# Three chunks of half products in the first MLP product of layer 0 as well, modulation pieces moved, and an output projection that opens four groups

## The chip, the cores and the metric

One core of a Trainium2 chip runs the whole program in one launch. The metric is the device time of a run in microseconds. TensorE (PE in the views) multiplies, VectorE (DVE) and ScalarE (ACT) do the work around it, GpSimd (POOL) issues some transfers, and SyncE (SP) issues the weight transfers.

## What is computed

The reference is one step of a two-layer backbone over 128 context tokens and 512 latent tokens, together T = 640 columns, with 1024 features. Cut to the parts that matter here:

```python
def layer(x, mod, lp, ...):
    shift1, scale1, gate1, shift2, scale2, gate2 = jnp.split(mod, N_MOD, axis=-1)
    hn = rmsnorm(x, lp['norm_w'][0]) * (1.0 + scale1) + shift1
    y, k, v, hs = mixer(hn, lp, ...)          # four head groups, then @ lp['w_out']
    x = x + gate1 * y
    hn = rmsnorm(x, lp['norm_w'][1]) * (1.0 + scale2) + shift2
    x = x + gate2 * (jnp.square(jax.nn.relu(hn @ lp['w_mlp1'])) @ lp['w_mlp2'])
```

`mod` comes from a product of a conditioning vector with `w_ada` (1024 x 6144) in each layer; `w_mlp1` is 1024 x 4096 and `w_mlp2` is 4096 x 1024. All of it is float32.

## The kernel before

**Layout.** Activations stand with features on the 128 partitions and the 640 tokens along the free axis, cut in two halves A and B, mostly 320 each. A float32 product is made of three matmuls in a reduced format: both sides are split into a high part and a remainder (`wh`, `wl` for weights; `hh`, `hl` for the normed activations), and high by high, remainder by high and high by remainder are added up in PSUM. One group is 8 slices of 128 features by 3, which is 24 matmuls of 320 columns (`group`, L768). ScalarE makes `wh` (L269, L314) and VectorE the remainder `wl` (L252), both for 128x1024 elements at a time.

**Stages.** Layers are numbered 0 and 1 in the code and here. After the mixers and the output projection (`g_L_o`), the MLP runs in four chunks q of 1024 inner features: a first product (MLP1, 16 groups, with squares by ScalarE and VectorE at L1460 to L1465), then its share of the second product (MLP2, 16 groups `g_L_0A` to `g_L_1B`, added to `x` by VectorE at L1404).

**Half products.** For the chunks in `FAST`, which are q = 1, 2, 3 of layer 1, `fast_mlp1` (L391) replaces four quarter products by seven products of sums: each pair of weight blocks needs 14 x 24 instead of 16 x 24 matmuls over the chunk (L432). `sums_gen` (L332) makes the sums of the activations once in a layer, after the first MLP1 chunk: for each of four slices there are twelve VectorE operations on 128x320 elements (the sums at L354 and L373 to L385, and remainders at L360 and L363) and four ScalarE casts. `sum_and_split` (L297) makes the sums of the weights, with an addition on VectorE (L311) before some of the splits. The products' results are added by VectorE at L450.

**Modulation.** The vector `mod` of layer 0's last third and of all of layer 1 is made on VectorE in passes over pieces of `w_ada` (`ada_dve`, L488 and L490): a piece is 512 KB and takes four passes of 128x512. There are 56 such pieces in the MLP of layer 0.

**Order of the work.** `run` writes a list of weight pieces in the order of their use, with modulation pieces among them. Five staging buffers `st` (`WST`) and four pairs `wh`, `wl` are in turn; a transfer on SyncE starts when a staging buffer is done with. In each chunk of layer 0 the pieces are dealt out so:

```python
n = 2 if q else AQ[b]          # behind each of four MLP1 weight blocks; AQ = (0, 1, 3, 5)
...
it += nxt[ni:ni + 2]           # behind each of four MLP2 weight blocks
```

The scheduler turns this into one fixed queue for each engine; an engine works through its queue in order. PSUM has two rotating banks for groups (`gp`), a tile `S` of three banks, and `TA`, `TB` and `U`. The output projection starts when two groups can be open; the last mixer outputs `y` that it needs come from VectorE and from a small product at L1244.

Of the kernel before, what the change touches and what calls it, by code (L numbers as in the profile page):

```python
# [9 lines left out]
F32 = mybir.dt.float32  # L10
F32R = mybir.dt.float32r
# [29 lines left out]
AQ = (0, 1, 3, 5)  # L41
AP1 = {"xr": (0, 8), "xb": (8, 16)}
WST = 5
FAST = {(1, 1), (1, 2), (1, 3)}
RP = 645
XC = 642
UP = 643
# [69 lines left out]
class Net:  # L117
# [30 lines left out]
    def setup_consts(self, consts):  # L148
        nc, c = self.nc, self.const
        self.cst = c.tile([P, 164], F32, name="cst")  # L150
        nc.scalar.dma_start(self.cst, consts[:, 0:164])
        self.ident = self.cst[:, 0:128]
        self.inv = self.cst[:, 128:130]
        self.edge = self.cst[:, 130:162].rearrange("p (f j) -> p f j", f=2)
        self.consts = consts
        self.sel = c.tile([P, 2], F32, name="sel")
        selv = self.cst[:, 0:128].rearrange("p (j r) -> p r j", j=4)[:, 0:2, :]
        nc.vector.reduce_sum(self.sel, selv, AX.X)
        self.ones = c.tile([P, P], F32, name="ones")
# [9 lines left out]
        self.rgw = c.tile([P, 8, P], F32, name="rgw")  # L169
# [162 lines left out]
    def sums_gen(self):  # L332
# [2 lines left out]
            yield  # L335
        self.vsbS.put(self.vsb)
        self.osbS.put(self.osb)
        o, v, qk = self.osbS.get(F32R), self.vsbS.get(F32R), self.qk.get(F32R)
        ms = [self.m.get(F32R) for _ in range(5)]
        self.sum_own = (o, v, qk, ms)  # L340
        of, vf = o.rearrange("p a b -> p (a b)"), v.rearrange("p a b -> p (a b)")
        cut = lambda t, k: t[:, HC * k:HC * k + HC]
        T1 = [(cut(of, k), cut(vf, k)) for k in range(4)]
        T2 = [(cut(qk, k), cut(qk, 4 + k) if k < 3 else cut(ms[4], 0)) for k in range(4)]
        T4 = [(cut(ms[k // 2], k % 2), cut(ms[2 + k // 2], k % 2)) for k in range(4)]
# [44 lines left out]

    def fast_mlp1(self, l, q, put):  # L391
        nc = self.nc
        self.until(lambda: self.summed and self.psS.ok() and self.psB.ok() and self.pt.ok(2), "sums")
        S, tb = self.psS.get(), self.psB.get()
        g = [self.gp.tile([P, 512], F32, tag="g", name=f"f{q}_{i}") for i in range(2)]
        pairs = [(g[0], g[1]), (S[:, 0:512], S[:, 512:1024]), (S[:, 1024:1536], tb)]
        t1, t5 = self.pt.get(), self.pt.get()
        half = lambda t, mi: t[:, HC * mi:HC * mi + HC]
        left = {}

        def finish(m, c, r, mi, sign):
            hi, lo = put(m, c)
            v = half(r, mi)

            def late():
# [6 lines left out]
                left[id(r)] -= 1  # L412
                if not left[id(r)]:
                    self.e.put(r)

            self.spawn(late(), first=True)

        for b in range(2):
            Y, Z, X = pairs[b % 3], pairs[(b + 1) % 3], pairs[(b + 2) % 3]
            r = u2 = None  # L420
            for prod, bank in ((1, Y), (5, Z), (6, Y), (3, Z), (2, X), (7, Y), (4, Y)):
# [4 lines left out]
                for mi in range(2):  # L426
# [33 lines left out]
        self.pt.put(t1, t5)  # L460
        self.psS.put(S)
        self.psB.put(tb)

    def sums_done(self):
        o, v, qk, ms = self.sum_own
        self.osbS.put(o)
        self.vsbS.put(v)
        self.qk.put(qk)
        self.m.put(*ms)
        self.vsb, self.osb = self.vsbS.get(), self.osbS.get()  # L470

    def ada_dve(self, l, s, g, kp):
        nc = self.nc
# [285 lines left out]
    def group(self, W, mi, mov, korder, ncols, nm):  # L759
# [3 lines left out]
        for i, k in enumerate(korder):  # L763
# [507 lines left out]
    def layer(self, l, last):  # L1271
# [118 lines left out]
        self.until(lambda: len(self.y) == 8 and not self.gens, "mixers")  # L1390
        self.mix_done = True
        self.until(lambda: (l, 1) in self.ada_done)

        self.until(lambda: self.m.ok(2), "acc")
        acc, rr = self.m.get(), self.m.get()
# [29 lines left out]
        self.gemm(self.order([(L, "o", b) for b in range(4)], lambda i: i == 2), mov_y,  # L1425
                  lambda key, mi, c, pt: ev(key, mi, c, pt, fin1), pre=lambda i: self.until(lambda: (l, 2, 0) in self.ada_done) if i == 12 else None)
# [20 lines left out]
        for q in range(4):  # L1447
# [288 lines left out]
    def run(self):  # L1736
# [3 lines left out]
        for l in range(DEPTH):  # L1740
# [71 lines left out]
```

## Time and profile before

| what | value |
| --- | --- |
| median of 3 runs | 1458.77 us (1457.07 to 1461.47) |
| the profiled execution's own time | 1458.18 us |
| its span, first to last instruction | 1456.4 us |
| TensorE busy | 98% of the span |
| VectorE busy | 69% |
| ScalarE busy | 44% |

A row of the views names the line, the engine, the operation, the tile written, and the tiles read. Busy time is what an engine's instructions cover; an instruction's duration can overlap the start of the next on its engine. In a chain each piece is what the next one waited for.

### The profile page before, as it was taken

To read this page: it belongs to the slowest core of one execution; us is meant where nothing else is said; L and a number is where in the kernel's file an instruction comes from. 1 tells how busy PE (TensorE), PEld (TensorE's weight loads), DVE (VectorE), ACT (ScalarE), POOL (GpSimd) and SP (SyncE) were. 2 spreads that over 40 slices of the span, in tenths; PEclk is the share of its full clock that TensorE was granted. 3 is DMA by queue.
4 is the path that set the end of the run, shared out by engine and by line. 5 is a ranking of instruction groups with operands and counts; after the bars stand their busy time and mean duration, and the time that the engine had idled before them with its cause. 6 is when DMAs were issued, how large, how long until landed. Compare 5 with 4: busy or idle time off the path is not lost.

```text
span 1456.4 us, 24564 instructions
## 1 busy us (share of the span) xinstructions
PE 1434.4 (98%) x9847; PEld 1367.7 (94%) x9847; DVE 998.6 (69%) x1924; ACT 643.7 (44%) x1195; POOL 60.9 (4%) x104
## 2 busy tenths in 40 slices
PE   8999999999999999999999999999999999999998
PEld 6877989999999999999999999899999999999997
DVE  5565989898886686866359768947594644644653
ACT  5535794363124123214346577625442722722731
POOL 1121010010000000000002200000000000000000
PEclk8999999999999999999999999999999999999999
DMA  9686214535553543543224601221222432432401
GB/s 333 195 220 186 79 43 97 159 95 175 176 186 115 161 146 117 177 147 122 74 78 127 155 30 59 44 73 59 88 85 79 143 104 74 148 106 77 151 23 73
DMA packets 145465, 174.02 MB, mean 119 GB/s; under 512 B 10500, under 2 KB 120536, under 8 KB 145352
## 3 DMA queue, kind: packets, MB, share of 16 engines
q1 hardware_dynamic: 140760, 165.85, 37.2%
q0 software_dynamic: 4224, 6.45, 2.0%
q8 instruction: 77, 1.26, 0.4%
q14 instruction: 36, 0.29, 0.1%
q10 hardware_dynamic: 368, 0.16, 0.0%
HBM read 159.84 MB, written 3.15 MB: 112 GB/s over the span
## 4 chain that ended last, share of the span: by engine, by line
PE 88%; DVE 5%; DMA 3%; ACT 2%; issue 1%; SPq 0%; DVEq 0%; ACTq 0%
PE g_L_0A L768 13%; PE g_L_1A L768 13%; PE g_L_0B L768 12%; PE g_L_1B L768 12%; PE S L432 4%; PE g_L_o_0B L768 2%; PE g_L_o_1B L768 2%; PE g_L_v L1361 2%; PE g_L_o_0A L768 2%; DMA st<-in_w_mlp 2%; PE g_L_o_1A L768 2%; PE f L432 2%; PE TB L1025 1%; PE S L978 1%; PE U L1133 1%; PE U L289 1%
## 5 line engine op out<-in xcount | busy, mean ns | idle before, releaser
L252 DVE TENSOR_TENSOR wl<-st,wh 128x1024 fp32r<-128x1024 f32 x194 | 236.8, 1222 | 107.8 <-ACT wh L269 69.8
L269 ACT CAST wh<-st 128x1024 fp32r<-128x1024 f32 x156 | 163.6, 1049 | 225.8 <-PE g_L_1B L768 195.1
L768 PE MATMUL g_L_1A<-z,wh 128*128 128x320 f32 (+1 forms) x512 | 122.1, 315 | 0.0
L768 PE MATMUL g_L_0A<-z,wh 128*128 128x320 f32 (+1 forms) x512 | 121.9, 314 | 0.0
L768 PE MATMUL g_L_0B<-z,wh 128*128 128x320 f32 (+1 forms) x512 | 115.9, 306 | 0.0
L768 PE MATMUL g_L_1B<-z,wh 128*128 128x320 f32 (+1 forms) x512 | 115.9, 306 | 0.0
L768 PEld LDWEIGHTS g_L_1A<-z,wh 128*128 128x128 f32 x512 | 87.8, 188 | 2.5 <-issue 2.5
L768 PEld LDWEIGHTS g_L_0A<-z,wh 128*128 128x128 f32 x512 | 87.9, 188 | 0.8 <-ACT z L408 0.6
L768 PEld LDWEIGHTS g_L_1B<-z,wh 128*128 128x128 f32 x512 | 86.4, 189 | 0.3 <-DVE x L1404 0.2
L768 PEld LDWEIGHTS g_L_0B<-z,wh 128*128 128x128 f32 x512 | 86.4, 188 | 0.1
L490 DVE SCALAR_TENSOR_TENSOR m<-st,SC,m 128x512 f32<-128x512 f32 x112 | 79.7, 747 | 8.0 <-DMA st<-in_w_ada 8.0
L490 DVE SCALAR_TENSOR_TENSOR pt<-st,SC,pt 128x512 f32<-128x512 f32 x112 | 80.3, 746 | 0.5
L768 PE MATMUL g_L_0A<-z,wl 128*128 128x320 f32 (+1 forms) x256 | 80.0, 312 | 0.0
L768 PE MATMUL g_L_1A<-z,wl 128*128 128x320 f32 (+1 forms) x256 | 80.0, 312 | 0.0
L768 PE MATMUL g_L_1B<-z,wl 128*128 128x320 f32 (+1 forms) x256 | 78.7, 307 | 0.0
L768 PE MATMUL g_L_0B<-z,wl 128*128 128x320 f32 (+1 forms) x256 | 78.5, 307 | 0.0
L684 ACT ACTIVATE e<-x 128x320 f32<-128x320 f32 (+2 forms) x56 | 26.4, 471 | 117.1 <-DVE x L1404 116.7
L314 ACT CAST wh<-st 128x1024 fp32r<-128x1024 f32 x42 | 44.1, 1050 | 76.4 <-PE g_L_1B L768 69.8
L1464 DVE TENSOR_TENSOR e<-e 128x320 f32<-128x320 f32 x80 | 39.0, 488 | 48.1 <-ACT z L1461 47.9
L987 DVE TENSOR_REDUCE mx<-S 128x2 f32<-128x1280 f32 x32 | 47.6, 1487 | 19.7 <-PE S L978 19.6
L991 ACT ACTIVATE e<-S,mx 128x640 f32<-128x640 f32 x64 | 50.9, 801 | 6.5 <-DVE mx L988 5.8
L1404 DVE SCALAR_TENSOR_TENSOR x<-g_L_0B,mod,x 128x192 f32<-128x192 f32 (+1 forms) x64 | 21.3, 375 | 45.2 <-PE g_L_0B L768 44.8
(666 smaller groups left out, 4253.2 us busy)
## 6 DMA issues: line engine op xcount, KB each, us to landing
st<-in_w_mlp SPq DMA_DIRECT2D x146, 512.0 KB
st<-in_w_ada SPq DMA_DIRECT2D x80, 512.0 KB
st<-in_w_in SPq DMA_DIRECT2D x36, 512.0 KB
st<-in_w_out SPq DMA_DIRECT2D x16, 512.0 KB
z<-in_w_ada SPq DMA_DIRECT2D x24, 256.0 KB
z<-qk SPq DMA_DIRECT2D x32, 80.0 KB
z<-qk POOLq DMA_DIRECT2D x32, 80.0 KB, 4.1
xt<-in_x_sample SPq DMA_DIRECT2D x4, 512.0 KB
```

The lines of the kernel that those rows point to most:

```text
L252: eng.tensor_tensor(wl.rearrange("p k c -> p (k c)"), st, wh.bitcast(F32).rearrange("p k c -> p (k c)"), OP.subtract)
L269: nc.scalar.copy(wh.rearrange("p k c -> p (k c)"), st)
L314: nc.scalar.copy(wh.rearrange("p k c -> p (k c)"), st)
L432: nc.tensor.matmul(bank[mi][:, 0:HC], w[:, k, sl], x, start=(fresh and n == 0), stop=(n == 11), skip_group_check=not fresh)
L490: nc.vector.scalar_tensor_tensor(acc[:, 0:512], w, col, acc[:, 0:512], OP.mult, OP.add)
L684: nc.scalar.activation(s[:, 0:n], self.x[:, k, cs], AF.Square)
L768: nc.tensor.matmul(pt[:, 0:ncols], w[:, k % 4, sl], r, start=(n == 0), stop=(n == 23))
L987: nc.vector.tensor_reduce(mx[:, 0:2], ps[:, 128:1408].rearrange("p (s k) -> p s k", s=2), AX.X, OP.max)
L991: nc.scalar.activation(es[s], ps[:, 128 + 640 * s:768 + 640 * s], AF.Exp, bias=mx[:, 2 + s:3 + s], scale=sc, accum_out=self.sm[:, i, s:s + 1])
L1361: nc.tensor.matmul(pt[:, 0:256], a[:, k, ts], b[:, k % 4, :], start=(n == 0), stop=(n == 23))
L1404: nc.vector.scalar_tensor_tensor(self.x[:, m, a:b], pt[:, a - a0:b - a0], self.mod[l][:, gate + m, st:st + 1], self.x[:, m, a:b], OP.mult, ...
L1464: nc.vector.tensor_tensor(r[:, 0:n], r[:, 0:n], r[:, 0:n], OP.mult)
```

## The change

It does three things.

- `FAST` holds q = 1, 2, 3 of both layers. Layer 0 gets the sums and the seven products; their buffers are the tile `rgw` and three `m` tiles instead of five `m` tiles, and two more `m` tiles hold the first products' results (`self.first`) instead of the `pt` tiles, which the modulation uses. `acc` and `rr` are given back in between and taken again after chunk 3.
- The modulation pieces of layer 0's chunks are dealt out one behind an MLP1 block and three behind an MLP2 block (`ADAQ`), in place of two and two; in chunk 0 MLP1 keeps `AQ`, and MLP2 has three.
- The output projection of both layers opens its first four groups (`gemm_early`): two in the `gp` banks and two in `S`, with six of the eight slices of `y` (`EARLY`); slices 5 and 7 follow when they are there.

```diff
-FAST = {(1, 1), (1, 2), (1, 3)}
+EARLY = (0, 1, 6, 4, 2, 3)
+FAST = {(l, q) for l in range(2) for q in (1, 2, 3)}
+ADAQ = (1, 3)
...
-        o, v, qk = self.osbS.get(F32R), self.vsbS.get(F32R), self.qk.get(F32R)
-        ms = [self.m.get(F32R) for _ in range(5)]
+        o, v, w, qk = self.osbS.get(F32R), self.vsbS.get(F32R), self.rgwS.get(F32R), self.qk.get(F32R)
+        ms = [self.m.get(F32R) for _ in range(3)]
+        self.first = [self.m.get(), self.m.get()]
...
-        t1, t5 = self.pt.get(), self.pt.get()
+        t1, t5 = self.first
...
+    def gemm_early(self, seq, mov, evac, early, late, ready):
+        self.until(lambda: self.psS.ok() and all(k in self.y for k in early), "early")
+        S = self.psS.get()
+        banks = [self.gp.tile([P, 512], F32, tag="g", ...) for i in range(2)]
+        banks += [S[:, 512 * i:512 * i + 512] for i in range(3)]
...
+        for i in range(len(seq)):
+            part(i, early)
+        for k in late:
+            self.until(lambda: k in self.y, f"y{k}")
+        self.until(lambda: not self.gens, "mixers")
+        ready()
+        for i, (key, mi, c) in enumerate(seq):
+            part(i, late)
...
+        self.gemm_early(seq[:4], mov_y, evo, EARLY, [k for k in range(KT) if k not in EARLY], gate)
...
-            if q == 0 and (l, 1) in FAST:
-                self.summed = False
+            if q == 0:
+                self.until(lambda: (l, 1, 1) in self.norm_done, "norm2B")
+                self.m.put(acc, rr)
+                self.summed, self.open = False, 0
                 self.spawn(self.sums_gen())
...
-                    n = 2 if q else AQ[b]
+                    n = ADAQ[0] if q else AQ[b]
...
-                        it += nxt[ni:ni + 2]
-                        ni += 2
+                        it += nxt[ni:ni + ADAQ[1]]
+                        ni += ADAQ[1]
```

VectorE's queue moves in two places. The first is the first MLP2 product of layer 0 (chunk 0), up to the remainder `wl` of the second half of its second weight block, without which the groups of that block stop after 12 matmuls. Before (L490 is a modulation pass, L640 small parameter work):

```order
L640 SCALAR_TENSOR_TENSOR small1_108<-small1_108 128x4
L490 SCALAR_TENSOR_TENSOR pt1_31_3983<-st70_3935,SC_97,pt1_31_3983 128x512
L640 SCALAR_TENSOR_TENSOR small1_108<-small1_108 128x4
L490 SCALAR_TENSOR_TENSOR pt0_30_3982<-st70_3935,SC_97,pt0_30_3982 128x512
L640 SCALAR_TENSOR_TENSOR small1_108<-small1_108 128x4
L490 SCALAR_TENSOR_TENSOR pt1_31_3983<-st70_3935,SC_97,pt1_31_3983 128x512
L640 SCALAR_TENSOR_TENSOR small1_108<-small1_108 128x4
L252 TENSOR_TENSOR wl72_4115<-st72_3996,wh72_4114 128x1024
```

With the change (L497 is a modulation pass, L359 to L390 are the sums of the activations, L255 is the remainder):

```order
L497 SCALAR_TENSOR_TENSOR pt0_30_3995<-st71_4006,SC_97,pt0_30_3995 128x512
L497 SCALAR_TENSOR_TENSOR pt1_31_3996<-st71_4006,SC_97,pt1_31_3996 128x512
L383 TENSOR_TENSOR e2_89_4112<-e1_90_4113,e2_89_4112 128x320
L386 TENSOR_TENSOR e1_90_4113<-e1_90_4113 128x320
L359 TENSOR_TENSOR e2_89_4112<-hh_77,hl_78 128x320
L368 TENSOR_TENSOR hl_78<-e2_89_4112,hh_77 128x320
L365 SCALAR_TENSOR_TENSOR qk_4_3984<-e1_90_4113,qk_4_3984 128x320
L390 TENSOR_TENSOR e2_89_4112<-e1_90_4113,e2_89_4112 128x320
L359 TENSOR_TENSOR e0_91_4199<-hh_77,hl_78 128x320 x2
L368 TENSOR_TENSOR rgw_2_3983<-e2_89_4112,m1_62_3986 128x320
L255 TENSOR_TENSOR wl73_4197<-st73_4033,wh73_4196 128x1024
```

Between the parameter step (L623 before, L630 now) and this remainder there were 10 modulation passes and no sum; now there are 14 passes and 38 operations of the sums.

The second place is the first half of a short chunk. In layer 1, before, from the remainder for product 3 (the last digit of `wl` names the product) to the two evacuations of product 3 (L450):

```order
L252 TENSOR_TENSOR wl215_3_11854<-st212_11318,wh215_3_11853 128x1024
L252 TENSOR_TENSOR wl215_2_11890<-st215_11589,wh215_2_11889 128x1024
L252 TENSOR_TENSOR wl217_7_11924<-st216_11628,wh217_7_11923 128x1024
L311 TENSOR_TENSOR st220_11907<-st220_11907,st221_11943 128x1024
L252 TENSOR_TENSOR wl218_4_11966<-st218_11872,wh218_4_11965 128x1024
L450 TENSOR_TENSOR e1_235_11938<-S_36_11819,e2_234_11904 128x320
L411 TENSOR_TENSOR z11_206_11941<-e1_235_11938,z13_205_11940 128x320
L450 TENSOR_TENSOR e1_235_11938<-S_36_11819,e2_234_11904 128x320
```

In layer 0, with the change, from the second remainder of the same four on (L314 adds weight blocks, L457 evacuates):

```order
L255 TENSOR_TENSOR wl90_2_4761<-st90_4572,wh90_2_4760 128x1024
L497 SCALAR_TENSOR_TENSOR m5_69_4588<-st94_4742,SC_97,m5_69_4588 128x512
L497 SCALAR_TENSOR_TENSOR m4_68_4587<-st95_4782,SC_97,m4_68_4587 128x512
L497 SCALAR_TENSOR_TENSOR m5_69_4588<-st95_4782,SC_97,m5_69_4588 128x512
L255 TENSOR_TENSOR wl92_7_4804<-st91_4607,wh92_7_4803 128x1024
L497 SCALAR_TENSOR_TENSOR m4_68_4587<-st95_4782,SC_97,m4_68_4587 128x512
L497 SCALAR_TENSOR_TENSOR m5_69_4588<-st95_4782,SC_97,m5_69_4588 128x512
L255 TENSOR_TENSOR wl93_4_4849<-st93_4740,wh93_4_4848 128x1024
L457 TENSOR_TENSOR e0_94_4756<-S_20_4640,e1_93_4718 128x320
L314 TENSOR_TENSOR st97_4826<-st97_4826,st98_4871 128x1024
L417 TENSOR_TENSOR z7_88_4759<-e0_94_4756,z6_87_4758 128x320
L457 TENSOR_TENSOR e0_94_4756<-S_20_4640,e1_93_4718 128x320
```

In layer 0 eight modulation passes stand in this stretch and just ahead of it, and the addition for the next half (`st97`, `st98`) now stands between the two evacuations. The same rows stand in the chunks q = 2 and 3.

## Rows read from the trace of the kernel before

**Rows 1.** The page, part 1 of the whole execution: busy us, share, instructions.
```profile
span 1456.4 us, 24564 instructions
...
PE 1434.4 (98%) x9847; PEld 1367.7 (94%) x9847; DVE 998.6 (69%) x1924; ACT 643.7 (44%) x1195; POOL 60.9 (4%) x104
```
**Rows 2.** The windows by stage; busy us and count of PE, PEld, DVE, ACT, POOL; clock; DMA.
```profile
355.00:413.90 58.90, 58.90 (x405) 57.79 (x403) 49.28 (x107) 11.01 (x15) 0.00 (x0) 1.00 0.54 163
413.90:471.50 57.60, 57.60 (x395) 56.56 (x395) 42.63 (x74) 22.00 (x39) 0.00 (x0) 1.00 0.46 145
...
1116.30:1168.80 52.50, 51.76 (x341) 49.74 (x340) 34.83 (x47) 35.88 (x68) 0.00 (x0) 1.00 0.42 131
```
**Rows 3.** The chain of waits, stretches of PE: start us, us, what.
```profile
370.00 3.53 PE g_L_0A L768 x24
...
1116.47 3.53 PE f L432 x24
...
1175.98 3.55 PE g_L_0B L768 x24
...
1225.47 3.52 PE f L432 x24
...
1284.08 3.56 PE g_L_0B L768 x24
```
**Rows 4.** The groups on DVE by shape: busy us, mean ns, idle before, releaser.
```profile
L252 DVE TENSOR_TENSOR wl<-st,wh 128x1024 fp32r<-128x1024 f32 x194 | 236.8, 1222 | 107.8 <-ACT wh L269 69.8 <-ACT wh L314 37.5
L490 DVE SCALAR_TENSOR_TENSOR pt<-st,SC,pt 128x512 f32<-128x512 f32 x112 | 80.3, 746 | 0.5
...
L311 DVE TENSOR_TENSOR st<-st,st 128x1024 f32<-128x1024 f32 x24 | 29.3, 1222 | 21.3 <-DMA st<-in_w_mlp 21.2
...
L354 DVE TENSOR_TENSOR e<-hh,hl 128x320 f32<-128x320 f32 x16 | 7.4, 485 | 0.1
```
**Rows 5.** The timeline of DVE at the first MLP2 product of layer 0.
```profile
353.99 1.23 DVE L252 TENSOR_TENSOR wl<-st,wh 128x1024 fp32r<-128x1024 f32 x1 [1.46 <-ACT wh L269]
356.54 0.23 DVE L623 TENSOR_TENSOR e<-e 128x64 f32<-128x64 f32 x1 [1.33 <-DMA e<-in_diff_lambda]
...
357.47 0.48 DVE L1464 TENSOR_TENSOR e<-e 128x320 f32<-128x320 f32 x1
357.88 0.75 DVE L490 SCALAR_TENSOR_TENSOR pt<-st,SC,pt 128x512 f32<-128x512 f32 x1
...
365.05 0.74 DVE L490 SCALAR_TENSOR_TENSOR pt<-st,SC,pt 128x512 f32<-128x512 f32 x1
365.71 0.15 DVE L640 SCALAR_TENSOR_TENSOR small<-small 128x4 f32<-128x4 f32 x1
...
367.26 1.22 DVE L252 TENSOR_TENSOR wl<-st,wh 128x1024 fp32r<-128x1024 f32 x1
368.39 0.67 DVE L1404 SCALAR_TENSOR_TENSOR x<-g_L_0B,mod,x 128x192 f32<-128x192 f32 x2
```
**Rows 6.** The timeline of PE after a wait in the first layer's projection.
```profile
93.66 0.87 PE L978 MATMUL S<-z,z 128*128 128x384 f32 x2 [2.15 <-DMA z<-qk]
```
**Rows 7.** The windows around that wait, columns as in Rows 2.
```profile
90.00:95.00 5.00, 2.85 (x16) 2.62 (x15) 1.22 (x1) 1.47 (x2) 0.06 (x1) 0.85 0.91 214
95.00:100.00 5.00, 5.00 (x30) 5.00 (x29) 0.63 (x1) 0.43 (x1) 0.00 (x0) 0.81 0.67 163
```
**Rows 8.** The chain inside the first short chunk of layer 1.
```profile
1122.68 4.99 DMA st<-in_w_mlp
...
1130.15 0.03 DVE e L450
1130.17 5.47 DMA st<-in_w_mlp
```
**Rows 9.** The waits of PE: releaser, us in total, times, longest.
```profile
PE U L1244 <- DVE z L1247: 2.5, 2, 2.2
```

More of the change, by code (lines that the diff above doesn't have):

```diff
@@ L168, in setup_consts @@
         self.SC = c.tile([P, KT, 32], F32, name="SC")
-        self.rgw = c.tile([P, 8, P], F32, name="rgw")
+        self.rgwS = Slots(c, ["rgw"], [P, 8, P])
+        self.rgw = self.rgwS.get()
         self.plw = c.tile([P, 2, P], F32, name="plw")
@@ L337, in sums_gen @@
         self.osbS.put(self.osb)
-        o, v, qk = self.osbS.get(F32R), self.vsbS.get(F32R), self.qk.get(F32R)
-        ms = [self.m.get(F32R) for _ in range(5)]
-        self.sum_own = (o, v, qk, ms)
-        of, vf = o.rearrange("p a b -> p (a b)"), v.rearrange("p a b -> p (a b)")
+        self.rgwS.put(self.rgw)
+        o, v, w, qk = self.osbS.get(F32R), self.vsbS.get(F32R), self.rgwS.get(F32R), self.qk.get(F32R)
+        ms = [self.m.get(F32R) for _ in range(3)]
+        self.first = [self.m.get(), self.m.get()]
+        self.sum_own = (o, v, w, qk, ms)
+        of, vf, wf = (t.rearrange("p a b -> p (a b)") for t in (o, v, w))
         cut = lambda t, k: t[:, HC * k:HC * k + HC]
         T1 = [(cut(of, k), cut(vf, k)) for k in range(4)]
-        T2 = [(cut(qk, k), cut(qk, 4 + k) if k < 3 else cut(ms[4], 0)) for k in range(4)]
-        T4 = [(cut(ms[k // 2], k % 2), cut(ms[2 + k // 2], k % 2)) for k in range(4)]
+        T2 = [(cut(qk, k), cut(qk, 4 + k) if k < 3 else cut(ms[2], 0)) for k in range(4)]
+        T4 = [(cut(ms[k // 2], k % 2), cut(wf, k) if k < 3 else cut(ms[2], 1)) for k in range(4)]
         A, B = slice(0, HC), slice(HC, T)
@@ L392, in fast_mlp1 @@
         nc = self.nc
-        self.until(lambda: self.summed and self.psS.ok() and self.psB.ok() and self.pt.ok(2), "sums")
+        self.until(lambda: self.summed and self.psS.ok() and self.psB.ok(), "sums")
         S, tb = self.psS.get(), self.psB.get()
@@ L403, in finish @@
             v = half(r, mi)
+            self.open += 1
             def late():
@@ L412, in late @@
                 left[id(r)] -= 1
+                self.open -= 1
                 if not left[id(r)]:
@@ L464, in sums_done @@
     def sums_done(self):
-        o, v, qk, ms = self.sum_own
+        o, v, w, qk, ms = self.sum_own
         self.osbS.put(o)
         self.vsbS.put(v)
+        self.rgwS.put(w)
         self.qk.put(qk)
-        self.m.put(*ms)
-        self.vsb, self.osb = self.vsbS.get(), self.osbS.get()
+        self.m.put(*ms, *self.first)
+        self.vsb, self.osb, self.rgw = self.vsbS.get(), self.osbS.get(), self.rgwS.get()
     def ada_dve(self, l, s, g, kp):
@@ L772, in group, with part @@
         return pt
+    def gemm_early(self, seq, mov, evac, early, late, ready):
+        nc = self.nc
+        self.until(lambda: self.psS.ok() and all(k in self.y for k in early), "early")
+        S = self.psS.get()
+        banks = [self.gp.tile([P, 512], F32, tag="g", name=f"g_{seq[i][0][0]}_e{i}") for i in range(2)]
+        banks += [S[:, 512 * i:512 * i + 512] for i in range(3)]
+        def part(i, ks):
+            key, mi, c = seq[i]
+            W = self.weights(key)
+            sl = slice(mi * P, mi * P + P)
+            for k in ks:
+                wh, wl = W[k // 4]
+                hi, lo = mov(k, c)
+                for n, (w, r) in enumerate(((wh, hi), (wl, hi), (wh, lo))):
+                    nc.tensor.matmul(banks[i][:, 0:self.wd(c)], w[:, k % 4, sl], r,
+                                     start=(k == early[0] and n == 0), stop=(k == late[-1] and n == 2))
+            self.tick()
+        for i in range(len(seq)):
[6 more added lines that the diff above has]
+            part(i, late)
+            if i == len(seq) - 1:
+                self.release(key)
+            with self.tc.high_priority(offset=OFF):
+                evac(key, mi, c, banks[i])
+            self.tick()
+        self.psS.put(S)
     def gemm(self, seq, mov, evac, korder=range(KT), pre=None):
@@ L1389, in layer @@
         self.mix_tail = True
[L1390 to L1395, printed above, removed]
+        acc = rr = None
         self.c0 = CUT[4 * l + 2]
@@ L1423, in mov_y, with gate @@
             return self.y[k][0][:, cs], self.y[k][1][:, cs]
-        self.gemm(self.order([(L, "o", b) for b in range(4)], lambda i: i == 2), mov_y,
-                  lambda key, mi, c, pt: ev(key, mi, c, pt, fin1), pre=lambda i: self.until(lambda: (l, 2, 0) in self.ada_done) if i == 12 else None)
+        seq = self.order([(L, "o", b) for b in range(4)], lambda i: i == 2)
+        evo = lambda key, mi, c, pt: ev(key, mi, c, pt, fin1)
+        def gate():
+            nonlocal acc, rr
+            self.mix_done = True
+            self.until(lambda: self.m.ok(2), "acc")
+            acc, rr = self.m.get(), self.m.get()
+            self.until(lambda: (l, 1) in self.ada_done)
+        self.gemm_early(seq[:4], mov_y, evo, EARLY, [k for k in range(KT) if k not in EARLY], gate)
+        self.gemm(seq[4:], mov_y, evo,
+                  pre=lambda i: self.until(lambda: (l, 2, 0) in self.ada_done) if i == 8 else None)
         for k in range(8):
@@ L1485, in layer @@
                           evac1, pre=pre1)
-            if q == 0 and (l, 1) in FAST:
-                self.summed = False
+            if q == 0:
+                self.until(lambda: (l, 1, 1) in self.norm_done, "norm2B")
+                self.m.put(acc, rr)
+                self.summed, self.open = False, 0
                 self.spawn(self.sums_gen())
-            if q == 3 and (l, 3) in FAST:
-                self.until(lambda: not self.gens, "last sums")
+            if q == 3:
+                self.until(lambda: not self.open, "last sums")
                 self.sums_done()
+                if not last:
+                    nc.gpsimd.memset(self.rgw, 0.0)
+                acc, rr = self.m.get(), self.m.get()
             if q == 0 and not last:
```

1 line of the change is left out of this document (removed).

## Prediction

> **What bounds the kernel now.** I read the shares of the engines first: TensorE is busy 1434.4 of 1456.4 us, VectorE 998.6, ScalarE 643.7 [rows 1]. A matmul taken away from TensorE is therefore worth its time wherever its weights and operands still come in time. The windows by stage say where they do: the first MLP2 product of layer 0 and the chunk behind it have no idle time on TensorE (58.90 of 58.90, 57.60 of 57.60), and VectorE is busy 49.28 and 42.63 there [rows 2]. So layer 0's MLP can only gain by fewer matmuls, and VectorE has some 9 us to spare in the first of the two stages and 15 in the second. Then the chain gives the price of a group: 24 matmuls take 3.53 us, 0.147 each [rows 3].
>
> All sums are made against the profiled execution's own time, 1458.2; the median of the runs stands 0.6 above it, and I add that at the end. No change means within 0.3%, 4.4 us, about what a measurement of this kernel can tell.
>
> **Matmuls removed.** The first MLP product of a chunk needs 14 x 24 matmuls where it had 16 x 24, which is 48 fewer. Three chunks of layer 0 make 144, by 0.147 [rows 3] 21.2 us, all on the path: **-21.2**.
>
> **Projection.** TensorE waits for the last small product of the mixers 2.5 us in two waits, the longest 2.2 [rows 9]. With four groups open it has 4 x 18 matmuls before it needs the last two slices, which covers both waits; the clock lost behind them can add a little. Bounds 0 and 3.4, taken: **-3.0**.
>
> **The sums of the activations, chunk 0.** This is the term that decides. They are 48 operations on VectorE with 128x320 elements, and the scheduler puts most of them into the first MLP2 product of layer 0, together with 12 modulation pieces in place of 8. VectorE's queue starts there at 356.5, when the parameters have landed [rows 5]; that step isn't changed. An operation on VectorE overlaps its predecessor, so I count from start to start [rows 5]: a modulation pass 0.66 (365.05 to 365.71), an operation of 320 elements 0.41 (357.47 to 357.88), a remainder 1.13 (367.26 to 368.39), an addition to `x` 0.34 (0.67 for two), a small one about 0.08 (half of its 0.15). Up to the remainder of the second block's second half the new queue holds
>
> - 14 passes: 9.2
> - 38 operations of the sums, 2 opening passes and 2 of the squares, 42 by 0.41: 17.2
> - the remainder: 1.1
> - 6 additions to `x`: 2.0
> - some 25 small ones: 2.0
>
> 31.5 in all, so the remainder is ready at 388.0. Before, the same remainder was written by 368.5 [rows 5]. TensorE starts that block at 370.00 and does 24 matmuls in 3.53 us [rows 3] without it, then stops at 373.5: a wait of **14.5**. (The alternative, that the sums wait for nothing and lie in idle time, would need 18 us of idle VectorE before 373.5, and the timeline has none between 356.5 and 368.4 [rows 5].)
>
> Next late is the third block. From 388.0 TensorE has 72 matmuls, 10.6, and wants the block's first remainder at 398.6. In VectorE's queue it stands behind the additions of the fourth group (0.6), four passes (2.6) and itself (1.1), and that group ends only at 398.6: ready at 402.9, **4.3** of waiting. Behind it the queue has only passes and remainders, and VectorE catches up.
>
> A long wait also costs clock. After TensorE's wait of 2.15 us in the projection [rows 6] the granted clock was 0.85 and 0.81 in the two windows of 5 us [rows 7]; full speed is 2.4 GHz and the lower level 1.2, so about 3.4 us went by at the lower level, and half of that, 1.7, was lost. One such fall or two, taken as 2. Together 14.5 + 4.3 + 2 = **+20.8**, bounds 14.5 and 24.
>
> The rule that VectorE drains its pipe after each operation before the next one starts (the Trainium skill, VectorE: DVE Perf Modes, The DRAIN you can't avoid) would have the 89 operations cost their full durations, about 0.08 more each, and so 7 us more of waiting; the time would then be 1489. The same page of the Trainium skill says that an operation that isn't held starts earlier. The starts in [rows 5] go by this second rule, pass after pass, so the first one gets no chance of its own.
>
> **The short chunks in layer 0.** In layer 1 a short chunk runs from 1116.47 to the `g_L_0B` row at 1175.98, and from 1225.47 to 1284.08 [rows 3]. Without two groups of the second product (7.06) and the 336 matmuls (49.4) there are 3.1 and 2.2 us of loss left, 2.7 in the mean. The short window itself shows TensorE idle for 0.7 of it and 341 matmuls [rows 2]. So a short chunk is never free of loss even where VectorE is busy only 34.83 of 52.50 [rows 2].
>
> Layer 0 adds modulation. Its four pieces make 16 passes, 10.6 us, so VectorE would be busy some 45 of 52: as a sum it fits, and the place in the queue is what counts. Eight passes, 5.3 us, stand before product 3's first evacuation. In layer 1 that evacuation comes at 1130.15 [rows 8], 13.7 after the chunk's start, when TensorE has done nearly four groups (14.1): 0.4 of slack. So it is **4.9** late. The second evacuation now stands behind the addition of two weight blocks. The transfer for that addition can only start when the remainder of product 7 frees its staging buffer; it takes 4.99 to 5.47 [rows 8], here 5.2, and VectorE waits for such transfers in layer 1 already (21.2 in all, 24 additions [rows 4]). From that remainder the first evacuation is done after two passes, a remainder and itself, 2.8; the second after 5.2 + 1.1 + 0.4 + 0.4 = 7.1. That is 4.3 apart, and TensorE has at most a group of 3.53 to do meanwhile: 0.8 to 1.6, taken **1.2**.
>
> A chunk then loses 2.7 + 4.9 + 1.2 = 8.8, and three lose **+26.4**. Lower bound: layer 1's better chunk, 2.2 x 3 = 6.6. Upper: both evacuations late by a whole transfer and a remainder (5.2 + 1.2 [rows 4, 8]), 2.7 + 12.8 = 15.5, times three 46.5.
>
> **Edits that cost nothing.** In the MLP2 products of chunks 1 and 2 twelve pieces take the place of eight, 16 passes or 10.6 us more on top of at most 49.28 in 58.90 [rows 2]; that fits just, and what covers it is the length of the product: were TensorE faster there, the passes would show. ScalarE's casts, the clearing of `rgw` by GpSimd and the other tiles for the first results lie on engines that are busy less than half of the time. SyncE's queue carries the same weight bytes; its pieces only come in another order.
>
> **Sum:** 1458.2 - 21.2 - 3.0 + 20.8 + 26.4 = 1481.2, and with the 0.6 **1482**.
>
> **Rivals.**
>
> *The chunks are like layer 1's.* The passes fill the time in which VectorE waits for transfers anyway (37.5, 69.8 and 107.8 us stand in its rows as idle [rows 4]), and the evacuations stay where they were: 2.7 x 3 = 8.1 in place of 26.4. 1458.2 - 24.2 + 20.8 + 8.1 + 0.6 = 1463.5, on the edge of no change. For it: in layer 1 the same queue is idle a third of the chunk. Against it: the passes stand right ahead of the evacuation, with buffers that come late.
>
> *Faster.* The one wait is that for the second block's remainder, 14.5; by the third block VectorE is ahead, and it then runs so far ahead that the chunks lose nothing. 1458.2 - 24.2 + 14.5 + 0.6 = 1449. It decides when all losses together stay under 24.2 - 4.4 = 19.8 us. For it: a queue with 56 fixed pieces has to get through them once, early or late. Against it: layer 1's chunks, without any passes, lose 2.2 to 3.1 each.
>
> *Every transfer is waited for.* The chunks cost their upper bound: 1458.2 - 24.2 + 20.8 + 46.5 + 0.6 = 1502. For it: five staging buffers serve weights and passes, and the passes give them back late. Against it: in most stages the transfer engines are busy about half of the time [rows 2].
>
> **How the numbers follow.** Forecast 0.53, chunks like layer 1's 0.22, faster 0.13, every transfer waited for 0.12. The second lies on the edge, half of it no change and half slower: faster 0.13, same 0.11, slower 0.53 + 0.11 + 0.12 = 0.76. The range goes from 1455, which leaves out the faster case (0.13), to 1499, which leaves out about half of the last (0.06).
>
> **What would show it.** In the trace of the changed kernel VectorE should work almost without a gap from 356.5 to about 388, while TensorE waits 13 to 16 us for one remainder, with a lower granted clock behind it; about 4 us of a second wait should stand at the third block; layer 0's three short chunks should take 57 to 60 us from the first `f` row to the second product where layer 1's take 52; TensorE should have 144 matmuls fewer, and the wait at the mixers' last product should be gone. I am wrong if that remainder is ready before about 376, if the short chunks of layer 0 take 53 or less, or if the time comes out under 1455.

## The result, and the profile after

The changed kernel takes 1467.76 us in the median (1465.42 to 1468.59), the kernel before 1458.62 beside it: a ratio of 1.0052, 95% interval 1.0039 to 1.0065. It is slower, as forecast, but by 9 us and not by 23. The profiled execution took 1465.4, 7.2 more than the one of before; the ledger below is of these two.

The page of the changed kernel, part 1, answers to [rows 1]:

```profile
span 1463.6 us, 24503 instructions
...
PE 1424.9 (97%) x9703; PEld 1350.1 (92%) x9703; DVE 1057.6 (72%) x2002; ACT 697.7 (48%) x1313; POOL 61.7 (4%) x105
```

TensorE has 144 matmuls fewer (9847 to 9703), and VectorE is busy 59 us longer. Next, windows of the whole MLP2 product of chunk 0 in layer 0, first before, then in the changed kernel, then two pieces of the latter (columns as in [rows 2]).

```profile
355.16:413.87 58.71, 58.71 (x402) 57.67 (x402) 49.09 (x107) 10.85 (x15) 0.00 (x0) 1.00 0.54 164
...
352.73:433.60 80.87, 65.44 (x401) 61.23 (x401) 75.53 (x164) 18.32 (x31) 0.00 (x0) 0.89 0.45 137
375.75:389.40 13.65, 6.37 (x18) 4.16 (x19) 12.26 (x26) 3.29 (x6) 0.00 (x0) 0.50 0.36 115
403.05:406.47 3.42, 3.42 (x15) 3.42 (x14) 3.42 (x6) 0.00 (x0) 0.00 (x0) 0.50 0.93 298
```

Before, this product took 58.71 us without any idle time on TensorE. Now it takes 80.87, of which TensorE is busy 65.44. VectorE is busy 75.53. In the two pieces the granted clock is 0.50, the lower level, and TensorE is busy 6.37 and 3.42 us.

The waits of TensorE in the whole execution (us in total, times, longest), the three largest of those in layer 0's MLP (of the third, 3.5 us lie there); the wait of [rows 9] has shrunk to 0.3:

```profile
PE U L509 <- DVE pt L497: 7.5, 1, 7.5
PE g_L_0A L775 <- DVE wl L255: 6.1, 2, 3.3
PE S L439 <- DVE e L457: 3.7, 5, 1.1
```

The timeline of TensorE in that product; the bracket is the idle time ahead of the row and what ended it:

```profile
370.57 0.39 PE L775 MATMUL g_L_1A<-z,wh 128*128 128x320 f32 x1 [1.09 <-DVE x L1440]
...
380.19 2.58 PE L509 MATMUL U<-pt,ones 128*32 128x512 f32 x4 [7.48 <-DVE pt L497]
385.61 0.63 PE L775 MATMUL g_L_0A<-z,wl 128*128 128x320 f32 x1 [2.84 <-DVE wl L255]
...
398.72 0.38 PE L775 MATMUL g_L_1A<-z,wh 128*128 128x320 f32 x1 [0.72 <-DVE x L1440]
402.40 0.41 PE L775 MATMUL g_L_0A<-z,wl 128*128 128x320 f32 x1 [3.30 <-DVE wl L255]
```

And VectorE's timeline there, from the parameter step to the first remainder and to the next two:

```profile
353.96 0.23 DVE L630 TENSOR_TENSOR e<-e 128x64 f32<-128x64 f32 x1 [0.74 <-DMA e<-in_diff_lambda]
...
383.95 0.47 DVE L368 TENSOR_TENSOR rgw<-e,m 128x320 fp32r<-128x320 f32 x1
384.35 1.21 DVE L255 TENSOR_TENSOR wl<-st,wh 128x1024 fp32r<-128x1024 f32 x1
...
398.49 2.73 DVE L497 SCALAR_TENSOR_TENSOR m<-st,SC,m 128x512 f32<-128x512 f32 x4
401.13 2.35 DVE L255 TENSOR_TENSOR wl<-st,wh 128x1024 fp32r<-128x1024 f32 x2
```

From 353.96 VectorE works through its queue without a gap and writes the remainder that TensorE lacks at 384.35 to 385.5. The five idle times of TensorE add up to 15.4. Four matmuls into `U`, the product over the modulation pieces, stand ahead in TensorE's queue and wait first; they split one long wait, from 372.7 to 385.6, into two.

The lengths of the chunks of layer 0 from the first matmul of the MLP1 product to the first of the next stage. Windows of the kernel before, chunks 1 and 3 (chunk 2 is as chunk 1, 116.08), then of the changed kernel, chunks 1, 2 and 3:

```profile
413.87:529.94 116.07, 116.07 (x795) 114.00 (x794) 83.41 (x142) 31.69 (x50) 0.00 (x0) 1.00 0.47 145
...
646.02:762.22 116.20, 116.20 (x792) 114.65 (x791) 65.59 (x117) 41.97 (x72) 0.78 (x1) 1.00 0.33 99
```

```profile
433.60:546.62 113.02, 111.00 (x746) 106.97 (x745) 96.67 (x152) 47.32 (x84) 0.00 (x0) 1.00 0.58 177
546.62:659.38 112.76, 111.06 (x747) 107.03 (x746) 96.90 (x152) 47.28 (x84) 0.00 (x0) 1.00 0.59 178
659.38:770.73 111.35, 111.35 (x744) 107.60 (x743) 71.86 (x118) 57.52 (x106) 7.27 (x11) 1.00 0.39 122
```

| term | forecast | measured in the two traces |
| --- | --- | --- |
| 144 matmuls fewer | -21.2 | -21.2 by count and 0.147 |
| projections | -3.0 | -3.6 (2.5 in layer 0, 1.1 up to the end of layer 1's) |
| MLP2 of chunk 0 | +20.8 | +22.2 (15.4 waiting; 6.7 longer busy, 4.9 of it by the lower clock) |
| losses of the three chunks | +26.4 | +10.0 (7.06 less 3.05, 3.32 and 4.85) |
| sum | +23.0 | +7.4 (the executions: +7.2) |

### The profile page after: what moved, and what is told of

Its sections match the earlier page's. It is cut to its first block, busy times and chain, and to the rows that moved or that the text cites. A ratio compares the mean times of both kernels' runs of the same rounds, so it can differ in the third digit from the quotient of the medians.

```text
span 1463.6 us, 24503 instructions
## 1 busy us (share of the span) xinstructions
PE 1424.9 (97%) x9703; PEld 1350.1 (92%) x9703; DVE 1057.6 (72%) x2002; ACT 697.7 (48%) x1313; POOL 61.7 (4%) x105
## 4 chain that ended last, share of the span: by engine, by line
PE 77%; DVE 10%; DMA 6%; issue 5%; ACT 2%; SPq 0%; DVEq 0%; ACTq 0%; POOLq 0%
PE S L439 9%; PE g_L_0A L775 8%; PE g_L_1A L775 8%; PE g_L_0B L775 7%; PE g_L_1B L775 7%; PE f L439 5%; DMA st<-in_w_mlp 3%; PE g_L_v L1402 2%; DVE pt L497 2%; PE g_L_o_0B L775 1%; PE TB L439 1%; DVE wl L255 1%; PE g_L_o_0A L775 1%; PE g_L_o_1A L775 1%; PE g_L_o_1B L775 1%
## 5 line engine op out<-in xcount | busy, mean ns | idle before, releaser
L255 DVE TENSOR_TENSOR wl<-st,wh 128x1024 fp32r<-128x1024 f32 x212 | 258.6, 1222 | 106.4 <-ACT wh L272 55.1
L272 ACT CAST wh<-st 128x1024 fp32r<-128x1024 f32 x132 | 138.5, 1049 | 145.7 <-PE g_L_1B L775 71.7
L317 ACT CAST wh<-st 128x1024 fp32r<-128x1024 f32 x84 | 88.2, 1050 | 141.4 <-PE g_L_1B L775 94.8
L775 PE MATMUL g_L_0A<-z,wh 128*128 128x320 f32 (+1 forms) x512 | 125.8, 321 | 0.0
L497 DVE SCALAR_TENSOR_TENSOR m<-st,SC,m 128x512 f32<-128x512 f32 x112 | 79.0, 745 | 4.9 <-DMA st<-in_w_ada 4.9
L497 DVE SCALAR_TENSOR_TENSOR pt<-st,SC,pt 128x512 f32<-128x512 f32 x112 | 79.3, 743 | 0.3
L691 ACT ACTIVATE e<-x 128x320 f32<-128x320 f32 (+2 forms) x56 | 26.4, 472 | 109.7 <-DVE x L1440 109.2
L314 DVE TENSOR_TENSOR st<-st,st 128x1024 f32<-128x1024 f32 x48 | 58.6, 1221 | 27.0 <-DMA st<-in_w_mlp 26.7
L439 PE MATMUL S<-hh,wh 128*128 128x320 f32 x192 | 61.9, 322 | 4.1 <-DVE e L457 3.7
L1028 DVE TENSOR_REDUCE mx<-S 128x2 f32<-128x1280 f32 x32 | 47.6, 1486 | 18.8 <-PE S L1019 18.6
L439 PE MATMUL S<-hl,wh 128*128 128x320 f32 x192 | 59.3, 309 | 0.0
```

Of the source, the lines that this page charges most:

```text
L255: eng.tensor_tensor(wl.rearrange("p k c -> p (k c)"), st, wh.bitcast(F32).rearrange("p k c -> p (k c)"), OP.subtract)
L272: nc.scalar.copy(wh.rearrange("p k c -> p (k c)"), st)
L314: nc.vector.tensor_tensor(st, st, self.held[add][0], OP.add)
L317: nc.scalar.copy(wh.rearrange("p k c -> p (k c)"), st)
L439: nc.tensor.matmul(bank[mi][:, 0:HC], w[:, k, sl], x, start=(fresh and n == 0), stop=(n == 11), skip_group_check=not fresh)
L497: nc.vector.scalar_tensor_tensor(acc[:, 0:512], w, col, acc[:, 0:512], OP.mult, OP.add)
```

## The experiments

Theory A says that the order of VectorE's queue costs the 22 us; theory B, that VectorE simply has too much work in that stage, 75.5 us beside some 58 of TensorE. Rivals are named with each run. Each run was compared with the kernel before on its own chip, where that kernel took 1460 to 1461; so I go by the ratios, with 1458.6 us for 1. By its ratio the changed kernel is 7.6 us slower than the one before (9.1 by the medians).

**x1, the projection as before.** The edit:

```diff
-        self.gemm_early(seq[:4], mov_y, evo, EARLY, ..., gate)
-        self.gemm(seq[4:], mov_y, evo, ...)
+        self.until(lambda: len(self.y) == 8 and not self.gens, "mixers")
+        gate()
+        self.gemm(seq, mov_y, evo, ...)
```

> The projection's first four groups are not opened early; all else as in the changed kernel. Theory (the projections gave 2.5 us in layer 0 and 1.1 in layer 1, by the shift of TensorE's stages between the two traces): 3.6 us longer than the changed kernel, about 1471.4, and the wait for the last small product of the mixers is back, 2 to 2.5 us. Rival (what TensorE gains there is only handed on to the wait for the remainder in the first MLP2 product, whose queue on VectorE begins with a transfer that starts at its own time): no more than 1 us from 1467.8.

Measured: 1471.79, ratio 1.0073 (1.0054 to 1.0092), 3 us above the changed kernel; the two intervals overlap, so the time alone doesn't decide. The trace does: the wait is back, and the MLP2 product of chunk 0 begins 2.1 us later than in the changed kernel (352.73) and ends 3.8 later (433.60), so the gain isn't handed on to that product's wait, as the rival has it.

```profile
PE U L1285 <- DVE z L1288: 2.5, 2, 2.2
...
354.86:437.43 82.57, 67.25 (x403) 62.78 (x402) 76.56 (x164) 18.85 (x32) 0.00 (x0) 0.88 0.43 135
```

**x4, the projection alone.** `FAST = {(1, q) for q in (1, 2, 3)}` and `ADAQ = (2, 2)`.

> Chunks of half products in layer 1 alone and modulation pieces two and two, as before; only the projection that opens four groups is kept of the change. Theory: 3.6 us less than before, 1455.0. Rival (the gain in layer 1's projection of 1.1 is another effect of the shifted order): 1456.1, and no change at all, 1458.6, if the early groups only pay where the MLP behind them is short of VectorE.

Measured: 1456.19, ratio 0.9964 (0.9951 to 0.9977), 5.3 us less than before. The early groups pay on their own, by the 3.6 of the traces or a little more. The second rival, no change, is out; the first one's 1456.1 lies just above the interval, which by the ratio is 1451.5 to 1455.2.

**x2, the remainders first.** The edit, in the function that gives the splits of weights their priority:

```diff
+        if key[0][0] == "L0" and k[0] == "2" and k[2] == 0:
+            return 400
```

> Only the order of the queues changes: the splits of the weights of layer 0's first MLP2 product get a higher priority, so the remainder that TensorE waited for stands 24 rows behind the one before it on VectorE and not 86. Theory A (the order in the queue costs the time; the sums themselves find room later): the wait of 12 us and most of the clock loss behind it go, a wait of 3 to 5 stays at the third block, and the time falls by 14 to 18 to 1450 to 1454. Theory B (VectorE has more work in this stage than TensorE, whatever the order): the wait only moves to the third block and to the first product with sums, the clock loss stays, and the time is 1463 to 1468.

Measured: 1463.84, ratio 1.0022 (1.0009 to 1.0035): 4.4 us less than the changed kernel. Windows of x2: chunk 0's MLP2 product, then the first product of chunk 1; below them TensorE's waits in both together.

```profile
355.17:427.49 72.32, 65.33 (x401) 59.06 (x401) 65.90 (x152) 16.29 (x28) 0.00 (x0) 0.98 0.38 120
427.49:490.76 63.27, 59.44 (x372) 54.93 (x370) 56.82 (x83) 39.48 (x74) 0.00 (x0) 0.97 0.63 194
```

```profile
PE g_L_0A L777 <- ACT wh L274: 2.4, 1, 2.4
PE f L441 <- DVE wl L257: 2.2, 1, 2.2
PE g_L_0B L777 <- DVE x L1442: 2.1, 2, 1.3
PE g_L_1B L777 <- DVE x L1442: 1.7, 1, 1.7
```

The product is 8.6 us shorter, and the chunk behind it 6.6 longer (63.27, in the changed kernel 56.66). VectorE's work is the same, 122.7 us in the two stages together (122.3 in the changed kernel), and the two take 135.6 where they took 137.5. The wait went where theory B put it, into several smaller ones further on; of theory A's 14 to 18 us little is left. By the ratio the time is 1461.8, 1.2 under theory B's range and 8 above theory A's. In one point B was wrong: most of the clock came back (0.98 and 0.97 in the two stages, 0.89 and 1.00 in the changed kernel).

**x3, no sums.** The sums in layer 0 are left out; the products read `hh` and `hl`.

```diff
+        if l == 0:
+            for p, k0, c in ((5, 0, A), (6, 4, A), (7, 0, B), (4, 4, B)):
+                self.Tsum[p] = [(self.hh[:, k, c], self.hl[:, k, c]) for k in range(k0, k0 + 4)]
+            self.summed = True
+            return
```

> Left out: the sums of the activations in layer 0 (48 operations on VectorE, 16 on ScalarE); the seven products there run on the plain activations, so the matmuls are the same in number. Theory A and B alike: VectorE reaches the remainder 38 x 0.41 = 15.6 us earlier, the wait is gone, chunk 0's MLP2 product takes 59 to 61 in place of 80.9, and the time is 1445 to 1449. Rival C (the modulation pieces that were moved there, and the wait of TensorE for their product into U, cost the time): the product still takes over 70 and the time stays above 1456.

Measured: 1445.91, ratio 0.9896 (0.9877 to 0.9915), 15 us less than before. Chunk 0's MLP2 product in x3:

```profile
354.52:413.82 59.30, 59.03 (x403) 57.47 (x402) 55.74 (x115) 10.77 (x14) 0.00 (x0) 1.00 0.60 187
```

59.30, as expected, with the twelve pieces and the product into `U` in it: rival C falls.

**x5 and x9, fewer pieces there.** The pieces of chunk 0's MLP2 product go to chunk 3's: x5 leaves one behind a block, x9 none.

```diff
-ADAQ = (1, 3)
+ADAQ = ((0, 1, 1, 1), (1, 3, 3, 2))
...
-                    n = ADAQ[0] if q else AQ[b]
+                    n = ADAQ[0][q] if q else AQ[b]
...
-                    if q < 3:
-                        it += nxt[ni:ni + ADAQ[1]]
-                        ni += ADAQ[1]
+                    it += nxt[ni:ni + ADAQ[1][q]]
+                    ni += ADAQ[1][q]
```

In x9 the second line is `ADAQ = ((0, 1, 1, 1), (0, 3, 3, 3))`.

> Only the dealing of the modulation pieces changes: in chunk 0's MLP2 product one behind each block in place of three, and the eight pieces go behind the MLP2 blocks of chunk 3. VectorE's work in chunk 0's product falls by 32 passes x 0.66 = 21 us, from some 75 to 54 us against 58 of TensorE, but the sums stay ahead of the remainder in the queue, behind two pieces (8 passes, 5.3 us) less. Theory A (order): a wait of 7 to 8 us for that remainder stays, the second is gone, chunk 0's product takes 68 to 70 where it took 80.9, the time is 11 to 13 us under the changed kernel, 2 to 4 under before. Theory B (the sum of the work): the wait is under 3, the time 8 or more under before. Rival C (the pieces don't matter, the sums alone do): no more than 4 us under the changed kernel.

> The changed kernel with no modulation piece in chunk 0's MLP2 product: the twelve go behind the MLP2 blocks of chunk 3, three each. With the runs before it makes a square: chunk 0's product takes 58.7 with neither sums nor more pieces, 59.3 with twelve pieces and no sums, 80.9 with both. Theory B (the sum of VectorE's work decides; either load alone fits beside TensorE): sums alone give 59 to 62, and the time is 9 to 13 us under before. Theory A (the queue's order: the sums stand ahead of the remainder in any case): a wait of 5 us or more stays, the product takes 65 or more and the time is at most 7 us under before.

Measured: x5 1450.51, ratio 0.9931 (0.9914 to 0.9947), 10 us less than before; x9 1446.56, ratio 0.9912 (0.9897 to 0.9927), 13 us less. The product in x5, then in x9:

```profile
355.39:417.81 62.42, 59.05 (x391) 58.44 (x390) 55.84 (x131) 17.21 (x29) 0.00 (x0) 0.97 0.38 119
```

```profile
355.92:413.01 57.09, 57.09 (x389) 57.09 (x390) 46.98 (x117) 17.20 (x30) 0.00 (x0) 1.00 0.33 100
```

In x5 one wait of 2.8 us for a remainder is left, in x9 none in this product. With that there are four corners: no sums and eight pieces, as before, 58.7 (VectorE 49.1); no sums and twelve pieces 59.3 (55.7); sums and no piece 57.1 (47.0; it has fewer products into `U` in it); sums and twelve pieces 80.9 (75.5). Sums with four pieces, x5, lie between (62.4; 55.8). The sums or the twelve pieces alone fit beside TensorE, both together don't. Theory B holds. x9 beats both kernels, with the half products in layer 0 and the early groups of the projection in it.

**x6, both edits.** x5's dealing and x2's priority.

> Both edits: the dealing of x5 and the remainders ahead of x2. If VectorE's queue order and the sum of its work in chunk 0 together make up the 22 us, chunk 0's product takes 59 to 61 with no wait over 1.5 us, and the time is that of the run without sums, 13 to 15 us under before. If transfers are the limit (a weight's transfer starts only when the pieces ahead of it have given back a staging buffer), a wait of 3 us or more for a cast stays in it and the time is 5 to 9 us under before.

Measured: 1452.90 (1447.69 to 1455.25), ratio 0.9950 (0.9932 to 0.9968), 7 us less than before. The product took 60.97, as the first theory said, with a longest wait of 1.9 where it allowed 1.5; but the time is the second's, and no wait for a cast stands behind it. The profiled execution was the fastest of the six; what the others lost isn't in its trace, and that stays open. It is not faster than x5.

**x7, plain additions on GpSimd.** `nc.gpsimd.tensor_tensor` in place of VectorE's in `full` (16 in a layer).

> The changed kernel with the 16 plain additions of the sums in each layer on GpSimd; the other 32 operations stay on VectorE. Theory B (VectorE's work): 16 x 0.41 = 6.6 us less on VectorE ahead of the remainder, some 13 of the 16 before it, so the wait falls by 5 and the time by 5 to 7. Rival: GpSimd takes over 1 us for each, every slice then waits for it, and the passes behind wait in the same queue: no gain, or slower than the changed kernel.

Measured: 1472.95, ratio 1.0082 (1.0061 to 1.0104): no gain. Chunk 0's MLP2 product in x7, then seven of GpSimd's additions, then rows of VectorE beside them:

```profile
353.02:434.89 81.87, 67.09 (x401) 61.83 (x402) 77.16 (x148) 18.10 (x30) 21.34 (x16) 0.90 0.43 135
```

```profile
355.32 4.03 POOL L359 TENSOR_TENSOR e<-hh,hl 128x320 f32<-128x320 f32 x4 [1.34 <-DVE z L1512]
...
366.49 3.90 POOL L359 TENSOR_TENSOR e<-hh,hl 128x320 f32<-128x320 f32 x3 [2.71 <-DVE small L647]
```

```profile
355.42 2.12 DVE L495 TENSOR_SCALAR pt<-st,SC 128x512 f32<-128x512 f32 x2
357.46 1.15 DVE L378 TENSOR_TENSOR e<-e 128x320 f32<-128x320 f32 x1
...
367.00 0.83 DVE L647 SCALAR_TENSOR_TENSOR small<-small 128x4 f32<-128x4 f32 x1
367.76 0.48 DVE L368 TENSOR_TENSOR rgw<-e,m 128x320 fp32r<-128x320 f32 x1
```

GpSimd takes 1.0 for each of the first four and 1.3 in the mean of all 16 (21.34), and VectorE waits for it only 0.8 us in this product. But while it adds, single operations of VectorE are 0.6 to 0.7 longer, large or small: 1.15 in place of 0.47 for 320 elements, 2.12 in place of 0.88 for two first passes (the kernel before, at 372.72), 0.83 in place of 0.15 for a small one. Others beside the same additions keep their length, as the one at 367.76 does. With 16 instructions fewer VectorE is busy longer (77.16) than in the changed kernel (75.53).

**x8, the price of passes in a short chunk.** x6 with `ADAQ = ((0, 0, 1, 2), (1, 3, 3, 2))`.

> As x6, but in the first products of the short chunks 1, 2 and 3 of layer 0 there are no, one and two pieces behind each block (one in all three before). It measures what the passes cost a short chunk. The prediction's price (a pass ahead of the evacuation makes it 0.66 later): from the first f to the second product 53.5 to 54 in chunk 1, 57 to 60 in chunk 2, 62 to 66 in chunk 3. Rival (the passes fill time in which VectorE waits for weight transfers anyway): 54, 55.5 to 56.5, 56 to 58. Against x6 the time would be 2 to 8 us longer by the first, within 2 us by the second.

Measured: 1452.23, ratio 0.9942 (0.9926 to 0.9959), the same as x6. From the first `f` to the second product in chunks 1, 2 and 3:

```profile
416.32:471.60 55.28, 55.15 (x361) 52.50 (x361) 42.40 (x61) 37.05 (x71) 0.00 (x0) 1.00 0.47 144
528.46:583.37 54.91, 53.94 (x357) 51.93 (x356) 49.41 (x73) 36.72 (x71) 0.00 (x0) 1.00 0.56 173
640.78:696.52 55.74, 55.07 (x352) 50.52 (x351) 50.88 (x77) 36.89 (x72) 1.37 (x2) 1.00 0.56 173
```

The three rows don't hold the same work, and the pieces didn't come where their number says. Of the matmuls 2, none and 8 go into `U`, and a set of two of them takes about as long as one of eight (1.0): 0.98, 0 and 3.11 us in all. With those and four small matmuls in chunk 3 (0.35) taken out, 359, 357 and 340 are left; at 0.147 each the losses are 1.5, 2.4 and 2.3. And ahead of product 3's first evacuation VectorE had no pass in chunk 1, eight in chunk 2 and eight in chunk 3; the rest came behind it. These are the evacuations:

```profile
429.94 0.48 DVE L459 TENSOR_TENSOR e<-S,e 128x320 f32<-128x320 f32 x1
542.28 0.48 DVE L459 TENSOR_TENSOR e<-S,e 128x320 f32<-128x320 f32 x1
654.44 0.49 DVE L459 TENSOR_TENSOR e<-S,e 128x320 f32<-128x320 f32 x1
```

They come 13.6, 13.8 and 13.7 after the start. Eight passes made the evacuation 0.2 later and the loss 0.9 larger, where the prediction's price is 4.9 for the evacuation alone. The rival's mechanism holds for eight passes; sixteen ahead of an evacuation are not shown by any run.

## Why the prediction was off by 14 us

**What held.** The path: matmuls off, VectorE's queue late in chunk 0's MLP2 product, projections a little shorter. The queue took 31.6 us from the parameter step to the end of the remainder (353.96 to 385.5) where 31.5 were counted from start to start. At full durations it would have been 7 us more. The Trainium skill (VectorE: DVE Perf Modes, The DRAIN you can't avoid) has both rules, that the next operation waits until the pipe is empty and that one that isn't held starts earlier; the trace agrees with the second. The third block's wait stands where it was put, 0.72 and 3.30 for 4.3. That this stage is the loss, and not the chunks, is what x3, x5 and x9 show by taking it away.

**Two sizes in that term, of opposite sign.** The waits were put at 14.5 + 4.3 = 18.8 and were 15.4. The long one lasted 12.9, since TensorE came to it later, after 1.09 for an addition to `x`; and 2.6 of it are covered by the matmuls into `U`. The clock was put at 2, from a wait of 2.15 us [rows 6, 7]. TensorE was busy 65.44 with 401 matmuls where 402 took 58.71, 6.7 longer. Of that the lower clock explains 4.9, half of the 6.37 and 3.42 us that TensorE was busy at 0.50. About 1 more is the product into `U`: its eight matmuls took 1.0 in one set before and come in two sets of four now, of which the second, at the full clock, takes 1.0 alone. The rest isn't placed. The fall behind a wait of 2 us isn't the price of a wait of 13 us with a second one behind it. That the whole term came out within 1.4 of the forecast is luck: 3.4 too much waiting stands against 4.7 too little busy time.

**The step that failed: "So it is 4.9 late", and with it 8.8 for a short chunk and +26.4 in the sum.** Eight passes, 5.3 us, were added in full to the time of the first evacuation. In layer 1 before, VectorE's rows from the chunk's start to that evacuation are these:

```profile
1120.00 1.23 DVE L252 TENSOR_TENSOR wl<-st,wh 128x1024 fp32r<-128x1024 f32 x1 [1.17 <-ACT wh L314]
1121.42 1.23 DVE L252 TENSOR_TENSOR wl<-st,wh 128x1024 fp32r<-128x1024 f32 x1 [0.20 <-ACT wh L314]
1125.74 1.23 DVE L252 TENSOR_TENSOR wl<-st,wh 128x1024 fp32r<-128x1024 f32 x1 [3.09 <-ACT wh L314]
1127.79 1.23 DVE L311 TENSOR_TENSOR st<-st,st 128x1024 f32<-128x1024 f32 x1 [0.82 <-DMA st<-in_w_mlp]
...
1130.07 0.48 DVE L450 TENSOR_TENSOR e<-S,e 128x320 f32<-128x320 f32 x1
```

They hold 1.17 + 0.20 + 3.09 + 0.82 = 5.3 us of idle time, as much as the passes take. The prediction read when the evacuation came, and not what VectorE did until then; the idle times of the whole execution [rows 4] stood under the rival. With the change, chunk 1 of layer 0 (start at 433.60):

```profile
436.69 1.41 DVE L497 SCALAR_TENSOR_TENSOR m<-st,SC,m 128x512 f32<-128x512 f32 x2 [0.58 <-DMA st<-in_w_ada]
...
443.06 1.42 DVE L497 SCALAR_TENSOR_TENSOR m<-st,SC,m 128x512 f32<-128x512 f32 x2 [1.36 <-DMA st<-in_w_ada]
...
447.99 0.48 DVE L457 TENSOR_TENSOR e<-S,e 128x320 f32<-128x320 f32 x1
450.33 1.23 DVE L314 TENSOR_TENSOR st<-st,st 128x1024 f32<-128x1024 f32 x1 [1.86 <-DMA st<-in_w_mlp]
...
451.88 0.48 DVE L457 TENSOR_TENSOR e<-S,e 128x320 f32<-128x320 f32 x1
```

Most of the passes lie in that idle time: 3.4 us of it are gone and 1.9 left. Another 1.1 is the addition that stood at 1127.79 in layer 1's queue and stands behind the first evacuation here. So the evacuation comes 14.4 after the start in place of 13.76 (1130.07 less 1116.31): 0.6 late, not 4.9. x8 shows the same in its own chunks, with 0.2. The second comes 3.9 behind it, held by the addition at 450.33 and its transfer, as forecast (4.3). TensorE's waits for the two are 1.8 in chunk 1, 1.7 in chunk 2 and none in chunk 3, where 4.9 + 1.2 = 6.1 were forecast. The losses are 4.0, 3.7 and 2.2 in place of 8.8 each, 10.0 in place of 26.4, a little above the rival "The chunks are like layer 1's" (8.1). What is left without these waits is 2.0 to 2.2 a chunk, near the 2.7 that was read from layer 1. Chunk 3 shows that this rest isn't waiting: TensorE is busy all of 111.35 us there, with matmuls that stand 0.150 apart in the mean and not 0.147.

The prediction's last sign also has a wrong reading in it. It says that layer 1's short chunks take 52 from the first `f` row to the second product; that was a window that ended inside the chunk. To the end of the last product's matmuls layer 1's chunks took 55.06, 54.17 and 54.46 before, and layer 0's take 56.66, 56.39 and 54.09. The first of each:

```profile
1116.31:1171.37 55.06, 54.32 (x358) 52.09 (x356) 35.80 (x49) 37.28 (x71) 0.00 (x0) 1.00 0.43 133
...
433.60:490.26 56.66, 54.65 (x362) 51.65 (x361) 46.78 (x71) 37.14 (x72) 0.00 (x0) 1.00 0.54 168
```

**The rivals.** "The chunks are like layer 1's" was nearest, in its mechanism too. Without the 0.6 it is 1462.9 against the profiled 1465.4: it lacks 4.7 of longer busy time in chunk 0 and 1.9 in the chunks, and has 3.4 of waiting too much and 0.6 too little gained in the projections. "Faster" failed on the clock, the further waits in chunk 0 and the chunks. "Every transfer is waited for" had 46.5 for the chunks where 10.0 were measured.

## What to carry to other kernels

Before an operation is charged with what stands ahead of it in its queue, subtract the idle time that the same stretch already has where the trace shows a like stage; only the excess delays it. Sum an engine's work over the stage before thinking of its order: 75 us beside 58 can't be ordered away (x2), but moved to a stage with room the pieces cost little (x9: its chunk 3, with twelve pieces more, takes 113.10, the changed kernel's 111.19 by the same marks). And price the clock by the length of the wait, with a row that has a wait of that length, or keep its bound wide.

## What was not expected of the hardware

GpSimd's additions slowed VectorE while they ran, by 0.6 to 0.7 us on single operations: 0.47 to 1.15 us for 320 elements, 0.44 to 1.06 for a first pass, 0.15 to 0.83 for a small one. The Trainium skill (GPSIMD Engine Reference, Specifications) says that GpSimd shares its interfaces to the on-chip memory with VectorE, with contention where VectorE has two inputs there or uses a two-port mode. x7 agrees in part, since operations with two inputs that ran beside the same additions kept their 0.48. At these sizes the move is a loss of VectorE's time.

And the lower clock cost more than the fall that the trace of before shows: it was at 0.50 from 375.75 to 389.40, inside and behind a wait of 13 us almost without matmuls, and again from 403.05 to 406.47, and cost 4.9 us in one stage with 15.4 us of waiting, where a wait of 2.15 had cost about 1.7 [rows 6, 7].
